# Transformer block with mLSTM and differential attention: second q and k groups and their heads ahead of convolutions and cells, idle steps behind GpSimd's roots, and w_out's first two sums kept outside PSUM

## The chip, the cores and the metric

The kernel runs on one core of a Trainium2 chip. The metric is the device time of one execution in microseconds (us), taken as the median of several runs. A core has TensorE (PE, with its weight loads listed apart as PEld), VectorE (DVE), ScalarE (ACT), GpSimd (POOL) and SyncE (SP); each takes its own instructions in the order in which they were issued, and they wait for each other through semaphores. All loads and stores of this kernel are issued by SyncE.

## What is computed

One block for 256 tokens of width 2048, in fp32. Cut to what matters here:

```
mod = silu(c) @ w_ada + b_ada            # six vectors of 2048
shift1, scale1, gate1, shift2, scale2, gate2 = split(mod, 6)
h = rms_norm(x) * (1 + scale1) + shift1
mq, mk, mv, mo, mi, mf, dq, dk, dv = split(h @ w_in)
mq, mk = silu(causal_dwconv([mq, mk]))                 # 4 taps
h_ml = rms_norm(mlstm_chunkwise(mq, mk, mv, mi, mf)) * sigmoid(mo)   # 4 heads
dq, dk = rope(rms_norm(dq)), rope(rms_norm(dk))        # 8 heads, two maps each
o_da = rms_norm(softmax(q1 k1) @ v - lam * softmax(q2 k2) @ v)
x = x + gate1 * ([h_ml, o_da] @ w_out)
g, u = split((rms_norm(x) * (1 + scale2) + shift2) @ w_gate_up)
out = x + gate2 * ((silu(g) * u) @ w_down)
```

## The kernel before

**Products.** Every large product goes through the same loop. A *tick* is a tile of weights, 128 x 1024. ScalarE copies the raw tile into a rounded high part `wh` (L211 in the profile, the line of the helper `act`), VectorE subtracts it from the raw tile and keeps the low part `wl` (L181, the helper `tt`), and TensorE makes twelve products of 128x128 by 128x512 with it (L581 `wh` by high activations, L582 `wl` by high, L583 `wh` by low), in two half ticks of six. There are 392 ticks: 12 column groups of w_in (two each for attention's q, k and v, one each for the mLSTM's q and k, two each for its v and output gate), w_out with 4 groups of 8, gate_up with 22 groups of 8, down with 4 of 22. Sums stand in two PSUM accumulators (`psA`) of 128 x 1024. All other PSUM work (transposes, scores, small sums) shares four banks (`psM`).

w_in is swept by pairs of k-blocks (`SWEEPS`): the groups in `EARLY` and `LATE` take turns, and a group's sum is added to its `proj` tile after each sweep. `EARLY` is the order of q, k and the mLSTM's q and k: dq0, dk0, mq, mk, dq1, dk1.

**The vectors of w_ada.** 192 tiles of 128 x 1024 are loaded by SyncE, four at a time. A tile is either multiplied by silu(c) and summed on VectorE (`ada`, L185, 128x1024) or used by TensorE (`gv`). `ADA_PLAN` gives for each stage how many tiles are due by which tick; more are taken by `ada_idle` when the planner holds VectorE's queue to be short enough.

**Everything else is woven between the half ticks.** A *work* is a Python generator; each `yield` ends a step and names the PSUM banks that the next step needs. `Plan.run` goes once through the list of works at each half tick, in the order in which they were added, and lets each work whose predecessors are done take one step, as long as the planner's own estimate of the queues of VectorE and ScalarE is below a limit. So the place in the list is a priority, and a step that only yields is a half tick in which that work issues nothing. A tick may need results (`ready`): `mix2` and `mix3`, attention's outputs for w_out's k-blocks 2 and 3, `mix0` and `mix1`, the mLSTM's, for blocks 0 and 1. When they have not been issued at that tick, `Plan.until` steps the works that are needed, and no product is issued in between.

The works near the change, in the order of the list: `q0`, `k0` (`prep`: root mean square, rotary products, eight transposes `tpk`), heads 0 to 3 (`attend`: scores `sc`, softmax `pm`, transposes `aT`; `attend_values`), `mix2` (`finish_attention`: roots `of`, one multiply of the 128x1024 tile `o`, eight transposes `ot`), the convolutions `conv0` and `conv1`, `q1`, `k1`, the cells of pair 0 (`ml_scores` with its score transposes `pp`, `ml_values`, `ml_norm` with its roots `mf`), heads 4 to 7 with `mix3`, the cells of pair 1, then for each pair `mg` (`ml_gate`: a sigmoid of the 128x1024 gate tile on ScalarE) and `mix0`/`mix1` (`ml_out`: four multiplies of `num`, eight transposes `mt`, high copies `mlh` and low parts `mll`), and `rows1` (`gate_rows`: gate1 as rows, four `g1rd` on VectorE and four sums `g1rp` on TensorE).

Reciprocal square roots are made by a first guess on VectorE (`rsqrt_first`) and three Newton rounds of four steps each on GpSimd (`rsqrt_newton`, L401 to L404 in the profile).

**w_out before.** Column groups 0 and 1 first take k-blocks 2 and 3 each, then 0 and 1 each: (g0: 2, 3), (g1: 2, 3), (g0: 0, 1), (g1: 0, 1); groups 2 and 3 follow whole. At the end of each group its sum is read from PSUM, multiplied by gate1's rows and added to x (`residual`, two steps on VectorE), so the last tick of each group needs `rows1`. Behind it stand the squares of the new x for the second norm (`x2_g`).

Of the kernel before, what the change touches and what calls it, by code (L numbers as in the profile page):

```python
# [14 lines left out]
AF = mybir.ActivationFunctionType  # L15
ALU = mybir.AluOpType
# [31 lines left out]
DQ, DK, DV, MQ, MK, MV, MO = (0, 1), (2, 3), (4, 5), 6, 7, (8, 9), (10, 11)  # L48
EARLY = (DQ[0], DK[0], MQ, MK, DQ[1], DK[1])
LATE = (DV[0], DV[1], MV[0], MV[1], MO[0], MO[1])  # L50
# [4 lines left out]
)  # L55
SQ0, SQ1 = True, False
FPAIRS = 6
FSWEEPS = ((0, 2), (2, 5), (5, 8))
# [106 lines left out]
def tile_block(ctx, tc, x, c, pos, par, w_ada, w_in, w_gt, w_out, w_gu, w_dn, out):  # L165
# [8 lines left out]
    plan = Plan()  # L174
# [73 lines left out]
    xs = {}  # L248
# [149 lines left out]

    def rsqrt_newton(y, b, x_):
        for _ in range(3):  # L400
            nc.gpsimd.tensor_tensor(b, y, y, op=ALU.mult)  # L401
            nc.gpsimd.tensor_tensor(b, b, x_, op=ALU.mult)
            nc.gpsimd.tensor_scalar(b, b, -0.5, 1.5, op0=ALU.mult, op1=ALU.add)
            nc.gpsimd.tensor_tensor(y, y, b, op=ALU.mult)  # L404
# [95 lines left out]
    accs = {}  # L500
# [227 lines left out]
    def prep(nm, g):  # L728
# [10 lines left out]
        rsqrt_first(dst, b, xx)  # L739
        rsqrt_newton(dst, b, xx)  # L740
        if nm == "q":
            nc.gpsimd.tensor_scalar(dst, dst, 0.125, None, op0=ALU.mult)
            rope_products(nm, t)
        else:
            yield 0
            v = t.rearrange("p (t m d) -> p t m d", t=2, d=64)
            for k in range(2):
                tt(v[:, k], v[:, k], dst[:, k].unsqueeze(2).to_broadcast([P, 8, 64]), ALU.mult)
            yield 0
            rope_products(nm, t)  # L750
# [80 lines left out]
    def finish_attention(g):  # L831
# [6 lines left out]
        rsqrt_first(f, b, xx)  # L838
        rsqrt_newton(f, b, xx)
        yield 0  # L840
        yield 0
        ov = osl[g].rearrange("p (h d) -> p h d", h=8)
# [149 lines left out]
    def ml_norm(g):  # L992
        h = slice(2 * g, 2 * g + 2)
        yield 0
        stt(mfx[:, h], mden[:, h], -1.0, mden[:, h], ALU.mult, ALU.max)
        tt(mfx[:, h], mfx[:, h], menm[:, h], ALU.max)
        stt(mfx[:, h], mfx[:, h], EPS, mfx[:, h], ALU.mult, ALU.mult)
        stt(mfx[:, h], mssq[:, h], 1.0 / 256, mfx[:, h], ALU.mult, ALU.add)
        rsqrt_first(mf[:, h], mfb[:, h], mfx[:, h])
        rsqrt_newton(mf[:, h], mfb[:, h], mfx[:, h])  # L1000
        yield 0
        yield 0

# [67 lines left out]
    def out_done(g):  # L1071
        def squares():
            yield 0
            for t in range(2):
                square_x(1, g, t)

        def go():
            residual(accs.pop(("wo", g)), rows1, g, xs[g], "o")
            plan.add(f"x2_{g}", squares())
        return go  # L1080
# [132 lines left out]
    mready = lambda kbs: [f"mix{kb}" for kb in kbs]  # L1213
    for g, kbs in ((0, (2, 3)), (1, (2, 3)), (0, (0, 1)), (1, (0, 1))):
        for kb in kbs:
            visit(("wo", g), kb == 2, kb == 1, mix, w_out[g], f"wo{g}", whole((kb,)), mready((kb,)),
                  out_done(g) if kb == 1 else None)
    for g in (2, 3):
# [108 lines left out]
    add_prep(0)  # L1327
    add_heads(0)
    plan.add("conv0", Lazy(conv, 0), fin(MQ))
    plan.add("conv1", Lazy(conv, 1), fin(MK))  # L1330
    add_prep(1)
    add_cells(0)
    add_heads(1)
    add_cells(1)
# [17 lines left out]
    for i, t in enumerate(ticks):  # L1352
# [23 lines left out]
        need = list(t["ready"])  # L1376
        if t["done"] and t["acc"][0] == "wo":
            need.append("rows1")
# [33 lines left out]

ADA_PLAN = ((0, 12, 3), (1, 16, 4), (2, 28, 0), (3, 8, 0), (4, 4, 0), (5, 4, 0), ("wo", 16, 22), ("f0", 24, 5), ("f1", 32, 5), ("f2", 8, 8))

# [70 lines left out]
```

## Time and profile before

| | |
|---|---|
| runs (us) | 1233.88, 1230.26, 1230.19; median 1230.26 |
| profiled execution (us) | 1227.86; its span 1226.1 |
| granted clock, mean | 0.992 |
| busy share: PE, DVE, ACT, POOL | 97%, 69%, 47%, 4% |
| DMA | 313.81 MB, mean 256 GB/s |

The profile is one execution: for each engine what it did when. Of the page, part 1 gives the busy share of each engine, and part 4 the chain of work that ended last, followed back from the last instruction to what released it. The other views are answers of the trace: busy time by stretches of time, groups of instructions by line and tile, the waits of one engine by what ended them, and the timeline, where a row is start, duration, engine, line, operation, output<-inputs, shapes, count, and in brackets the idle time ahead of it and what ended that. The starts of TensorE's products are measured and their ends are modelled.

### The profile page before, as it was taken

What the parts mean: (1) busy time and instruction counts of PE and PEld (TensorE: products, weight loads), DVE (VectorE), ACT (ScalarE), POOL (GpSimd) and SP (SyncE); (2) the same over time, 40 slices, a digit from 0 to 9 for tenths busy, and PEclk for the clock granted to TensorE, in tenths of its full rate; (3) what the DMA queues carried; (4) which work ended last, traced back from release to release, by engine and by line L of the source; (5) the groups of instructions that cost most, each with busy time, mean ns of one, the idle gap of its engine ahead of it and who ended that gap; (6) DMA issues with size and microseconds to landing.
All of it is one profiled execution on the core that took longest, in us unless ns stands there. A gap on an engine that the chain in (4) does not pass through costs nothing.

```text
span 1226.1 us, 14849 instructions
## 1 busy us (share of the span) xinstructions
PE 1189.7 (97%) x5590; PEld 955.9 (78%) x5590; DVE 851.1 (69%) x1197; ACT 582.1 (47%) x791; POOL 50.4 (4%) x126
## 2 busy tenths in 40 slices
PE   6999899998999898999999999999999999999998
PEld 2767678777888686788888888888888878888886
DVE  3757968898888998879856667878555454545443
ACT  3754345565666345665444444444444443433342
POOL 1000001205022000000000000000000000000000
PEclk9999999999999999999999999999999999999999
DMA  9898987656578897899755547998655544646471
GB/s 343 320 363 321 376 324 251 252 207 234 183 257 314 315 355 279 307 337 344 276 186 184 188 169 291 353 351 319 233 178 196 189 172 172 225 169 238 157 257 52
DMA packets 63258, 313.81 MB, mean 256 GB/s; under 512 B 6993, under 2 KB 7377, under 8 KB 41169
## 3 DMA queue, kind: packets, MB, share of 16 engines
q1 hardware_dynamic: 63186, 312.86, 69.9%
q8 instruction: 44, 0.72, 0.2%
q14 instruction: 28, 0.23, 0.0%
HBM read 310.73 MB, written 2.10 MB: 255 GB/s over the span
## 4 chain that ended last, share of the span: by engine, by line
PE 77%; DVE 13%; issue 3%; DMA 2%; POOL 2%; ACT 2%; SPq 0%; DVEq 0%; POOLq 0%; ACTq 0%
DVE wl L181 5%; DVE ada L185 4%; DMA ada<-in_w_ada_dram 2%; PE acc('dn', 0)_7816 L583 2%; PE acc('dn', 0)_7816 L581 2%; PE acc('dn', 2)_8616 L583 2%; PE acc('dn', 2)_8616 L581 2%; PE acc('dn', 1)_8236 L583 2%; PE acc('dn', 1)_8236 L581 2%; PE acc('dn', 0)_7816 L582 2%; PE acc('dn', 2)_8616 L582 2%; PE acc('dn', 1)_8236 L582 2%; DVE proj L181 1%; PE gv L216 1%; PE at L220 1%
## 5 line engine op out<-in xcount | busy, mean ns | idle before, releaser
L181 DVE TENSOR_TENSOR wl<-r,wh 128x1024 fp32r<-128x1024 f32 x392 | 473.6, 1221 | 206.6 <-ACT wh L211 206.3
L211 ACT ACTIVATE wh<-r 128x1024 fp32r<-128x1024 f32 x392 | 410.5, 1058 | 391.3 <-DMA r<-in_w_gu_dram 42.1
L185 DVE SCALAR_TENSOR_TENSOR ada<-ada,silc 128x1024 f32<-128x1024 f32 x152 | 183.0, 1217 | 1.7 <-DMA ada<-in_w_ada_dram 1.7
L216 PE MATMUL gv<-ada,early 128*32 128x256 f32 x320 | 25.7, 424 | 11.9 <-DMA ada<-in_w_ada_dram 11.7
L581 PE MATMUL acc('dn', 0)_7816<-wh,aTh 128*128 128x512 f32 x88 | 35.9, 408 | 0.0
L583 PE MATMUL acc('dn', 0)_7816<-wh,aTl 128*128 128x512 f32 x88 | 34.3, 390 | 0.0
L582 PE MATMUL acc('dn', 0)_7816<-wl,aTh 128*128 128x512 f32 x88 | 34.3, 389 | 0.0
L581 PE MATMUL acc('dn', 1)_8236<-wh,aTh 128*128 128x512 f32 x88 | 34.2, 389 | 0.0
L582 PE MATMUL acc('dn', 1)_8236<-wl,aTh 128*128 128x512 f32 x88 | 34.2, 389 | 0.0
L583 PE MATMUL acc('dn', 1)_8236<-wh,aTl 128*128 128x512 f32 x88 | 34.2, 389 | 0.0
L581 PE MATMUL acc('dn', 2)_8616<-wh,aTh 128*128 128x512 f32 x88 | 34.2, 389 | 0.0
L582 PE MATMUL acc('dn', 2)_8616<-wl,aTh 128*128 128x512 f32 x88 | 34.2, 389 | 0.0
L583 PE MATMUL acc('dn', 2)_8616<-wh,aTl 128*128 128x512 f32 x88 | 34.2, 389 | 0.0
L216 PEld LDWEIGHTS gv<-ada,early 128*32 128x32 f32 x320 | 7.8, 113 | 27.3 <-DMA ada<-in_w_ada_dram 16.4
L211 ACT ACTIVATE hx<-pt,modc,gcol 128x256 f32<-128x256 f32 (+1 forms) x36 | 17.4, 535 | 17.7 <-PE pt L220 14.6
L181 DVE TENSOR_TENSOR hl<-hx,hh 128x512 fp32r<-128x512 f32 (+1 forms) x18 | 11.4, 631 | 18.8 <-ACT hh L211 18.7
L211 ACT ACTIVATE pm<-sc,st,sclq 128x256 f32<-128x256 f32 (+1 forms) x32 | 15.9, 513 | 12.0 <-POOL st L785 12.0
L211 ACT ACTIVATE aTh<-at 128x512 fp32r<-128x512 f32 x22 | 12.0, 596 | 20.0 <-PE at L220 20.0
L211 ACT ACTIVATE fp<-fp 128x1024 f32<-128x1024 f32 x6 | 6.4, 1062 | 29.4 <-DVE fp L181 29.4
L582 PEld LDWEIGHTS acc('dn', 0)_7816<-wl,aTh 128*128 128x128 f32 x88 | 16.5, 188 | 4.2 <-issue 1.0
L581 PEld LDWEIGHTS acc('dn', 0)_7816<-wh,aTh 128*128 128x128 f32 x88 | 16.5, 188 | 4.2 <-issue 1.0
L582 PEld LDWEIGHTS acc('dn', 2)_8616<-wl,aTh 128*128 128x128 f32 x88 | 16.5, 188 | 3.5
(958 smaller groups left out, 2985.9 us busy)
## 6 DMA issues: line engine op xcount, KB each, us to landing
ada<-in_w_ada_dram SPq DMA_DIRECT2D x192, 512.0 KB, 5.7
r<-in_w_gu_dram SPq DMA_DIRECT2D x76, 1024.0 KB, 6.3
r<-in_w_dn_dram SPq DMA_DIRECT2D x44, 1024.0 KB, 4.8
r<-in_w_in_dram SPq DMA_DIRECT2D x36, 1024.0 KB, 6.7
r<-in_w_out_dram SPq DMA_DIRECT2D x16, 1024.0 KB, 7.4
r<-in_w_in_dram SPq DMA_DIRECT2D x24, 512.0 KB, 5.9
r<-in_w_gu_dram SPq DMA_DIRECT2D x24, 512.0 KB, 4.3
x<-in_x_dram SPq DMA_DIRECT2D x4, 512.0 KB, 5.9
```

Of the source, the lines that this page charges most:

```text
L181: nc.vector.tensor_tensor(o, a, b, op=op)
L185: nc.vector.scalar_tensor_tensor(out=o, in0=a, scalar=s, in1=b, op0=op0, op1=op1, accum_out=accum)
L211: nc.scalar.activation(o, a, func, **kw)
L216: nc.tensor.matmul(o, l, r, start=start, stop=stop, **kw)
L220: nc.tensor.transpose(o, a, ident[:])
L581: nc.tensor.matmul(o, ah[:, s], wh[:, r], start=t["start"] and j == 0, stop=False)
L582: nc.tensor.matmul(o, ah[:, s], wl[:, r], start=False, stop=False)
L583: nc.tensor.matmul(o, al[:, s], wh[:, r], start=False, stop=t["stop"] and j == 1)
```

## The change

- `EARLY` becomes dq0, dk0, dq1, dk1, mq, mk. In the list of works `q1`, `k1` and heads 4 to 7 with `mix3` now stand right behind `mix2`, ahead of the convolutions and of all cells.
- `behind(n)` makes a work yield n times without issuing anything. It stands behind the roots of k, of attention's output and of the cells: 7, 7 and 5 for the first group, 1 for the second. Before, these were 1, 2 and 2 steps for both.
- With `now=True`, for these three roots of the second group, the three Newton rounds run as nine steps on VectorE instead of twelve on GpSimd. In the order of instructions GpSimd has 95 rows where it had 131, VectorE 993 where it had 969 (like instructions in a row count once).
- w_out's groups 0 and 1 take turns block by block: 2, 3, 0, 1 of k, and for each g0, then g1. When one of them is complete, ScalarE copies its sum from PSUM into an SBUF slab (`wo0`, `wo1`), and the residual and the squares become a work that waits for `rows1`. Only groups 2 and 3 need `rows1` at their last tick.
- For w_out, `ADA_PLAN` spreads its 16 tiles up to 18 ticks before the stage's end instead of 22.

Line numbers from L57 on are one higher in the changed kernel, and 12 higher from the products on (L593 to L595).

```diff
-EARLY = (DQ[0], DK[0], MQ, MK, DQ[1], DK[1])
+EARLY = (DQ[0], DK[0], DQ[1], DK[1], MQ, MK)
...
+WORDER = (2, 3, 0, 1)
...
+    def behind(n):
+
+        for _ in range(n):
+            yield 0
+
+    def rsqrt_newton(y, b, x_, now=False):
+
         for _ in range(3):
+            if now:
+                tt(b, y, y, ALU.mult)
+                stt(b, b, -0.5, x_, ALU.mult, ALU.mult)
+                stt(y, b, 1.5, y, ALU.add, ALU.mult)
+                continue
...
-        rsqrt_newton(dst, b, xx)
+        rsqrt_newton(dst, b, xx, nm == "k" and g == 1)
...
-            yield 0
+            yield from behind(7 if g == 0 else 1)
...
-        rsqrt_newton(f, b, xx)
-        yield 0
-        yield 0
+        rsqrt_newton(f, b, xx, g == 1)
+        yield from behind(7 if g == 0 else 1)
...
-        rsqrt_newton(mf[:, h], mfb[:, h], mfx[:, h])
-        yield 0
-        yield 0
+        rsqrt_newton(mf[:, h], mfb[:, h], mfx[:, h], g == 1)
+        yield from behind(5 if g == 0 else 1)
...
+        def later():
+
+            kept = slab(f"wo{g}")
+            act(kept[:], accs.pop(("wo", g))[:], AF.Copy)
+            yield 0
+            yield 0
+            residual(kept, rows1, g, xs[g], "o")
+            yield from squares()
+
         def go():
-            residual(accs.pop(("wo", g)), rows1, g, xs[g], "o")
-            plan.add(f"x2_{g}", squares())
+            if g < 2:
+                w = later()
+                next(w)
+                plan.add(f"x2_{g}", w, ["rows1"])
+            else:
+                residual(accs.pop(("wo", g)), rows1, g, xs[g], "o")
+                plan.add(f"x2_{g}", squares())
...
-    for g, kbs in ((0, (2, 3)), (1, (2, 3)), (0, (0, 1)), (1, (0, 1))):
-        for kb in kbs:
-            visit(("wo", g), kb == 2, kb == 1, mix, w_out[g], f"wo{g}", whole((kb,)), mready((kb,)),
-                  out_done(g) if kb == 1 else None)
+    for kb in WORDER:
+        for g in (0, 1):
+            visit(("wo", g), kb == WORDER[0], kb == WORDER[3], mix, w_out[g], f"wo{g}", whole((kb,)), mready((kb,)),
+                  out_done(g) if kb == WORDER[3] else None)
...
     add_prep(0)
     add_heads(0)
+    add_prep(1)
+    add_heads(1)
     plan.add("conv0", Lazy(conv, 0), fin(MQ))
     plan.add("conv1", Lazy(conv, 1), fin(MK))
-    add_prep(1)
     add_cells(0)
-    add_heads(1)
     add_cells(1)
...
-        if t["done"] and t["acc"][0] == "wo":
+        if t["done"] and t["acc"][0] == "wo" and t["acc"][1] >= 2:
...
-ADA_PLAN = (..., ("wo", 16, 22), ...)
+ADA_PLAN = (..., ("wo", 16, 18), ...)
```

What this does to the order shows at three places.

On VectorE, in the part with the attention heads, the end of the first group: `of_269` are the root steps (the last two of the first guess; GpSimd's twelve follow on their own engine), `o` is the 128x1024 multiply that reads their result, `proj_518` and `rpk` are k's normalization and rotary products of the second group, `wl` a weight tile's low part. Before:

```order
L190 TENSOR_SCALAR of_269<-of_269 128x8
L192 TENSOR_SCALAR of_269<-of_269 128x8
L181 TENSOR_TENSOR proj_518<-proj_518,rstk 128x512 x2
L181 TENSOR_TENSOR rpk<-proj_518,rope_kc 128x128 x2
L181 TENSOR_TENSOR rpk<-proj_518,rope_ks 128x128 x2
L181 TENSOR_TENSOR proj_518<-rpk 128x16x8 x2
L181 TENSOR_TENSOR wl_2674<-r_2447,wh_2659 128x1024
L181 TENSOR_TENSOR o_2539<-o_2539,of_269 128x1024
```

After, the last eleven rows up to the same multiply; the first guess ends 27 rows ahead of it. `st` are the maxima of the next heads' scores:

```order
L186 SCALAR_TENSOR_TENSOR ada_5_2_2628,gsum<-ada_5_2_2628,silc_124 128x1024
L182 TENSOR_TENSOR wl_2828<-r_2660,wh_2798 128x1024
L197 TENSOR_REDUCE st_2830<-sc_0_2802 128x1
L197 TENSOR_REDUCE st_2830<-sc_1_2803 128x1
L197 TENSOR_REDUCE st_2830<-sc_0_2802 128x1
L197 TENSOR_REDUCE st_2830<-sc_1_2803 128x1
L197 TENSOR_REDUCE st_2836<-sc_0_2810 128x1
L197 TENSOR_REDUCE st_2836<-sc_1_2811 128x1
L197 TENSOR_REDUCE st_2836<-sc_0_2810 128x1
L197 TENSOR_REDUCE st_2836<-sc_1_2811 128x1
L182 TENSOR_TENSOR o_2586<-o_2586,of_269 128x1024
```

Between the first guess and the multiply there were five rows (nine instructions), and there are 26 now.

On TensorE, in w_out, the transposes `mt` of the first pair of cells, with products of attention's part (`odh`, `odl`) around them. Before:

```order
L583 MATMUL acc('wo', 0)_3396<-wh_3373,odl_3406 128x512
L220 MATMUL mt_3490<-ident,num_2915 128x128 x4
L220 MATMUL mt_3491<-ident,num_2915 128x128 x4
L581 MATMUL acc('wo', 0)_3396<-wh_3424,odh_3405 128x512
L582 MATMUL acc('wo', 0)_3396<-wl_3440,odh_3405 128x512
L583 MATMUL acc('wo', 0)_3396<-wh_3424,odl_3406 128x512
```

The first product that reads `mlh` stands 64 rows further on. After:

```order
L595 MATMUL acc('wo', 1)_3330<-wh_3425,odl_3224 128x512
L221 MATMUL mt_3576<-ident,num_3411 128x128 x4
L221 MATMUL mt_3577<-ident,num_3411 128x128 x4
L593 MATMUL acc('wo', 0)_3252<-wh_3474,mlh_3589 128x512
L594 MATMUL acc('wo', 0)_3252<-wl_3512,mlh_3589 128x512
L595 MATMUL acc('wo', 0)_3252<-wh_3474,mll_3590 128x512
```

The product that reads `mlh` now follows the transposes at once, and the third one reads `mll`.

On VectorE, the same place: `num` are the four multiplies that the transposes read, `mll` the low parts, `modc` and `ada` work for the vectors of w_ada, `g1rd` the diagonals for gate1's rows. Before:

```order
L185 SCALAR_TENSOR_TENSOR num_2915<-num_2915,mf,proj_655 128x256 x4
L181 TENSOR_TENSOR wl_3480<-r_3297,wh_3466 128x1024
L181 TENSOR_TENSOR modc<-gsum 128x16
L181 TENSOR_TENSOR modc<-modc,part 128x16
L185 SCALAR_TENSOR_TENSOR ada_0_1_3287,gsum<-ada_0_1_3287,silc_125 128x1024
L181 TENSOR_TENSOR wl_3511<-r_3297,wh_3488 128x1024
L185 SCALAR_TENSOR_TENSOR num_3343<-num_3343,mf,proj_689 128x256 x4
L185 SCALAR_TENSOR_TENSOR mll_3514<-mt_3490,part,mlh_3513 128x256 x2
L185 SCALAR_TENSOR_TENSOR mll_3514<-mt_3491,part,mlh_3513 128x256 x2
```

After:

```order
L186 SCALAR_TENSOR_TENSOR ada_0_0_3401,gsum<-ada_0_0_3401,silc_124 128x1024
L186 SCALAR_TENSOR_TENSOR ada_0_1_3446,gsum<-ada_0_1_3446,silc_125 128x1024
L182 TENSOR_TENSOR wl_3546<-r_3319,wh_3527 128x1024
L182 TENSOR_TENSOR g1rd_3552<-ident,modc 128x512
L186 SCALAR_TENSOR_TENSOR ada_0_2_3466,gsum<-ada_0_2_3466,silc_124 128x1024
L186 SCALAR_TENSOR_TENSOR num_3411<-num_3411,mf,proj_655 128x256 x4
L186 SCALAR_TENSOR_TENSOR ada_0_3_3504,gsum<-ada_0_3_3504,silc_125 128x1024
L186 SCALAR_TENSOR_TENSOR ada_1_0_3535,gsum<-ada_1_0_3535,silc_124 128x1024
L186 SCALAR_TENSOR_TENSOR ada_1_1_3538,gsum<-ada_1_1_3538,silc_125 128x1024
L186 SCALAR_TENSOR_TENSOR mll_3590<-mt_3576,part,mlh_3589 128x256 x2
L186 SCALAR_TENSOR_TENSOR mll_3590<-mt_3577,part,mlh_3589 128x256 x2
```

Ada steps now stand ahead of `num` and between `num` and `mll`, where a weight split and one ada step stood.

More of the change, by code (lines that the diff above doesn't have):

```diff
@@ L397, in rsqrt_first @@
         ts(y.bitcast(I32), b.bitcast(I32), -1.0, 1597463007.0, ALU.mult, ALU.add)
-    def rsqrt_newton(y, b, x_):
+    def behind(n):
+        for _ in range(n):
+            yield 0
+    def rsqrt_newton(y, b, x_, now=False):
         for _ in range(3):
+            if now:
[3 more added lines that the diff above has]
+                continue
             nc.gpsimd.tensor_tensor(b, y, y, op=ALU.mult)
@@ L1410, in __next__ @@
         return next(self.gen)
-ADA_PLAN = ((0, 12, 3), (1, 16, 4), (2, 28, 0), (3, 8, 0), (4, 4, 0), (5, 4, 0), ("wo", 16, 22), ("f0", 24, 5), ("f1", 32, 5), ("f2", 8, 8))
+ADA_PLAN = ((0, 12, 3), (1, 16, 4), (2, 28, 0), (3, 8, 0), (4, 4, 0), (5, 4, 0), ("wo", 16, 18), ("f0", 24, 5), ("f1", 32, 5), ("f2", 8, 8))
 def _layout(a):
```

## The prediction

> **What bounds the kernel now.** First comes the chain of waits, part 4 of the page: three quarters of the span hang on TensorE (PE). Next the busy times by stretch tell where PE is not filled: 212 to 379 us is the end of the input projection with attention and the mLSTM cells beside it, 379 to 479 is w_out, and after 520 comes the feed-forward part.
>
> ```profile
> PE 77%; DVE 13%; issue 3%; DMA 2%; POOL 2%; ACT 2%; SPq 0%; DVEq 0%; POOLq 0%; ACTq 0%
> ```
>
> ```profile
> 212.00:379.00 167.00, 160.03 (x816) 130.80 (x815) 145.46 (x285) 103.15 (x231) 38.14 (x88) 0.99 0.63 224
> 379.00:479.00 100.00, 96.29 (x417) 76.95 (x415) 92.69 (x141) 48.47 (x68) 5.79 (x12) 0.98 0.90 340
> 520.00:1226.00 706.00, 701.51 (x3137) 579.04 (x3135) 435.64 (x464) 301.65 (x315) 0.00 (x0) 1.00 0.63 228
> ```
>
> The columns are length, busy PE, PEld, DVE, ACT and POOL with their counts, clock, DMA share, GB/s. After 520 us PE issues 3137 products in 706 us, 0.225 us each: that is full speed, and the change touches nothing there. In the two stretches before it VectorE (DVE) is 87% and 93% busy: there it can be the one that is late. The waits of PE from 205 to 520 us, in total, times and longest, name what it was late with:
>
> ```profile
> PE ot L220 <- DVE o L181: 4.2, 1, 4.2
> PE g1rp L216 <- DVE g1rd L181: 3.5, 1, 3.5
> PE acc('gu', 4, 0)_4423 L582 <- DVE wl L181: 1.3, 2, 1.0
> PE tpk L220 <- DVE proj L181: 1.3, 1, 1.3
> PE aT L220 <- ACT pm L211: 0.7, 1, 0.7
> PE sc L216 <- ACT pm L211: 0.5, 1, 0.5
> PE aT L220 <- ACT wh L211: 0.3, 1, 0.3
> ```
>
> These seven rows are the most that the change can win. What each is worth shows in the starts on PE's timeline, since ends are modelled and a stall is followed by a slow stretch:
>
> ```profile
> 225.75 0.39 PE L583 MATMUL acc('in', 7, 4)_1961<-wh,hl 128*128 128x512 f32 x1
> 227.44 1.09 PE L220 MATMUL tpk<-ident,proj 128*128 128x128 f32 x8 [1.29 <-DVE proj L181]
> 228.29 0.48 PE L581 MATMUL acc('in', 7, 4)_1961<-wh,hh 128*128 128x512 f32 x1
> ...
> 302.36 0.39 PE L583 MATMUL acc('in', 5, 2)_2530<-wh,hl 128*128 128x512 f32 x1
> 306.90 1.97 PE L220 MATMUL ot<-ident,o 128*128 128x128 f32 x8 [4.15 <-DVE o L181]
> 308.66 1.55 PE L220 MATMUL tpk<-ident,proj 128*128 128x128 f32 x8
> 309.97 0.48 PE L581 MATMUL acc('in', 5, 2)_2530<-wh,hh 128*128 128x512 f32 x1
> ...
> 414.36 1.02 PE L216 MATMUL g1rp<-g1rd,ones 128*128 128x512 f32 x2
> 418.90 2.02 PE L216 MATMUL g1rp<-g1rd,ones 128*128 128x512 f32 x2 [3.52 <-DVE g1rd L181]
> 419.93 1.42 PE L581 MATMUL acc('wo', 0)_3396<-wh,mlh 128*128 128x512 f32 x1
> 421.14 0.63 PE L582 MATMUL acc('wo', 0)_3396<-wl,mlh 128*128 128x512 f32 x1
> ...
> 422.39 0.39 PE L582 MATMUL acc('wo', 0)_3396<-wl,mlh 128*128 128x512 f32 x1
> ```
>
> Eight transposes by themselves take 0.85 us (227.44 to 228.29), a g1rp 1.02. So k's transposes lost 228.29 - 225.75 - 0.23 - 0.85 = **1.5 us**. Attention's transposes lost 309.97 - 302.36 - 0.23 - 1.7 = **5.7**, of which 1.4 is that the 16 transposes took 3.07 instead of 1.7. The gate rows lost 422.39 - 414.36 - 2.04 - four products at 0.225 = **5.1**.
>
> **Part by part: what goes.** The 4.15 us are GpSimd's: the multiply of o starts when its twelfth root step has ended.
>
> ```profile
> 305.39 0.20 POOL L404 TENSOR_TENSOR of<-of 128x8 f32<-128x8 f32 x1
> ```
>
> ```profile
> 305.62 1.22 DVE L181 TENSOR_TENSOR o<-o,of 128x1024 f32<-128x1024 f32 x1 [1.51 <-POOL of L404]
> ```
>
> With the seven idle steps this multiply stands 26 rows behind the roots in DVE's order, where before it stood five behind; seven of the 26 are 1024 wide, and such steps follow each other at 1.15 us:
>
> ```profile
> 408.86 1.22 DVE L185 SCALAR_TENSOR_TENSOR ada<-ada,silc 128x1024 f32<-128x1024 f32 x1
> 410.01 1.22 DVE L185 SCALAR_TENSOR_TENSOR ada<-ada,silc 128x1024 f32<-128x1024 f32 x1
> ```
>
> That is 8 us of cover from these alone, against a wait of 4.15. I take the 5.7 as gone, and the 1.5 of k in group 0 likewise. The second group's roots run on DVE and need no other engine. The gate rows are no longer awaited where w_out's first group ends, since its sum goes to SBUF: the 5.1 goes. Its price there is two ScalarE copies of 1024, behind which only weight splits queue. The three waits in attention come to 1.5 as listed, some 2 by starts, since a listed idle leaves out about 0.17 of the product's modelled end (0.39 against 0.225). They need not all go: a head's transposes stand 30 to 42 products behind its scores in either order. I take half, 1.1. The 1.3 in the feed-forward part goes too: the fourth block of normed columns is now transposed together with the third, so ScalarE no longer takes it up behind a projection's copy. Together 1.5 + 5.7 + 5.1 + 1.1 + 1.3 = **14.7 us**.
>
> **What comes.** All cells now stand behind all attention heads, so the last score transposes (pp) stand in w_out, and PE has just six products between them and the transposes mt of the first cell pair, and none between mt and the product that reads their result. That chain now stands on the path, twice. Its prices, by groups of DVE and of ACT (count, busy, mean ns, idle before):
>
> ```profile
> L181 DVE TENSOR_TENSOR wl<-r,wh 128x1024 fp32r<-128x1024 f32 x79 | 95.7, 1218 | 1.7 <-ACT wh L211 1.7
> L185 DVE SCALAR_TENSOR_TENSOR ada<-ada,silc 128x1024 f32<-128x1024 f32 x59 | 71.0, 1218 | 1.7 <-DMA ada<-in_w_ada_dram 1.7
> L185 DVE SCALAR_TENSOR_TENSOR num<-num,mf,proj 128x256 f32<-128x256 f32 x8 | 3.3, 478 | 1.5 <-POOL mf L404 1.5
> L185 DVE SCALAR_TENSOR_TENSOR mll<-mt,part,mlh 128x256 fp32r<-128x256 f32 x8 | 3.3, 475 | 0.0
> L181 DVE TENSOR_TENSOR g1rd<-ident,modc 128x512 f32<-128x512 f32 x4 | 2.7, 685 | 0.0
> L185 DVE SCALAR_TENSOR_TENSOR st<-rs,lam,st 128x2 f32<-128x2 f32 x8 | 1.8, 225 | 0.3
> ```
>
> ```profile
> L211 ACT ACT_TABLE_LOAD x6 | 7.7, 1283 | 1.8 <-DVE mneg L196 1.6
> L211 ACT ACTIVATE proj<-proj 128x1024 f32<-128x1024 f32 x2 | 2.0, 1052 | 0.0
> L211 ACT ACTIVATE mp<-pp 128x384 f32<-128x384 f32 x4 | 2.0, 496 | 3.2 <-PE pp L220 3.2
> ```
>
> First stall, ahead of mt: after the last pp ScalarE copies it (0.5), loads a table (1.28), takes the sigmoid (1.05), and DVE multiplies num four times (3.3/2 = 1.65): 4.5. PE has six products, 1.35: **3.1**. DVE's own queue over the same stretch, three ada steps, one split and a g1rd (5.3) with num behind, ends at about the same time, if DVE is some 2.5 us ahead of PE at that pp, which is an estimate from its count of steps up to there. Second stall, behind mt: DVE has three ada steps (3.45) queued ahead of the first mll (0.48); PE has the transposes and two products (1.3): **2.6**. With the slow stretch of 1.4 as behind ot: 3.1 + 2.6 + 1.4 = **7.1**. Second pair: DVE needs two splits, three ada steps, a g1rd, twenty small steps of 0.2 (the root steps that left GpSimd among them) and num, about 12.5 us in all; PE has 46 products at 0.225 and three fp32 blocks of 0.5 to 1, some 11.9: 0.6. Behind its mt again a split and two ada: 2.6. Half a ramp, 0.6. Together **3.8**. On top come thin covers: in group 1 the heads' last transposes, k's and o's each have about 1 us of slack by count; I put **0.7** there.
>
> The bounds: if DVE comes ahead and no ramp follows, the two places cost 4.5 and 2.9, no new stall elsewhere: 7.4. If ada transfers hold DVE, 16 and more. Everything else is hidden: the copies of w_out's sums and two more table loads lie in ScalarE's idle half (48.47 busy of 100), 27 root steps on DVE add 27 x 0.22 = 6 us spread over 200, of which the second pair's nine are counted. On SyncE's queue, which issues all loads, weights and ada tiles keep their order among themselves, but more tiles are called for in w_out's first half.
>
> One rule speaks about the table load: the Trainium skill, "ScalarE: Activation LUTs", section "What ACT_TABLE_LOAD costs", adds a drain of about 1.38 us to each switch. By it the first stall would be 1.4 longer and the change worth 1.7 instead of 3.1. The trace does not show it: six loads here have 1.8 us of idle ahead in all, not 8.
>
> The sum: 11.6 - 14.7 = **-3.1 us**. It is made against the profiled execution of 1227.86 us (span 1226.1), so 1224.8; the runs shown have a median of 1230.26, and I predict **1227.0** beside that. A measurement of this kernel tells about 0.3%, 3.7 us, from no change, so the forecast lies just inside that edge.
>
> **The rivals.**
> A, cheap chains. DVE reaches num early and the clock holds: the new stalls cost 7.4, the sum is -7.3, 1223. For it: the planner issues nothing new while it waits for a mix, so queues are short. Against it: the ramp follows shorter stalls in this trace, below. Chance 0.21.
>
> ```profile
> 164.79 0.64 PE L216 MATMUL gv<-ada,early 128*32 128x256 f32 x8 [1.78 <-DMA ada<-in_w_ada_dram]
> ...
> 167.27 0.63 PE L581 MATMUL acc('in', 9, 2)_1444<-wh,hh 128*128 128x512 f32 x1
> 167.70 0.63 PE L582 MATMUL acc('in', 9, 2)_1444<-wl,hh 128*128 128x512 f32 x1
> ```
>
> Here products follow at 0.43, half speed, behind a wait of 1.78. The Trainium skill, "TensorE: Matmul & The Clock Gate", Part 1, has the rate halved after an idle window of about 3.4 us. By that rule stalls of 3.1 and 2.6 would leave full speed and save 2.0, a sum of -5.1; the rows above disagree with it, so I leave the ramp in.
>
> B, attention gets tight. Heads of both groups now run back to back, ScalarE and DVE alternate in them, and four PSUM banks serve all: if each of the four or five thin covers fails by 1 us, 4 to 5 us come back as waits of aT, tpk or ot on DVE and ACT. Then the sum is +1 to +2 and the time 1231, no change. The idle steps would do nothing that shows. For it: DVE at 87% already. Against: today's longest wait of aT or sc is 0.7. Chance 0.16.
>
> C, slower: the ada tiles. w_out already has the DMA rings at a share of 0.90 and 340 GB/s. The change calls for eleven tiles between the last pp and the second mll. DVE takes its queue in order, so a tile that has not landed holds num and mll behind it, and with them PE. It decides from the point where the new stalls pass 14.7 + 3.7 = 18.4. At one tile per 2.0 to 2.3 us instead of 1.2 (an estimate: 0.52 MB of tile with as much of weights beside it takes 3.1 us at 340 GB/s) eleven tiles are 9 to 12 us late: a sum of +6 to +9, say 1237. Against it: DVE waited 1.7 us in all for ada in 205 to 480 us. Chance 0.13.
>
> **How the numbers follow.** The forecast has 0.50 and a range of its own from 1223.5 to 1230; half of it lies under 1226.6, where faster begins. Faster: 0.25 + 0.21 = 0.46. Same: 0.25 + 0.16 = 0.41. Slower: 0.13. The range runs from 1220, for A with the attention waits gone too, to 1234, where C begins; it leaves out C and a little of A.
>
> **What would show it.** Right: in the waits of PE, ot and g1rp are gone, and two new rows stand at mt on num and at w_out's products on mll, 2 to 3 us each, with products at 0.43 behind them; POOL has 36 steps fewer. A shows as these rows under 1.5 us, B as new rows of aT, tpk or ot, C as DVE rows ada<-DMA of several us between pp and mll. I am wrong if ot or g1rp still stand there, or if the feed-forward part differs by more than 2 us.

## Result and profile after

The changed kernel takes 1221.89 us (median of 4 runs, 1221.63 to 1223.18) against 1232.07 us for the kernel before beside it: a ratio of 0.9918, with an interval from 0.9903 to 0.9933, so 8 to 12 us faster. A second comparison, below, gave 0.9939 (0.9919 to 0.9960). The profiled executions stand closer together: 1227.86 before, 1223.18 after (spans 1226.1 and 1221.5), 4.7 us.

Where the two traces part shows in the starts of the same products: the first of the last sweep over the groups in `EARLY`, the first of w_out's third group (nearly everything that the change moves lies between these two), and the first of gate_up's second sweep. Before, then after:

```profile
186.87 0.39 PE L581 MATMUL acc('in', 0, 4)_1621<-wh,hh 128*128 128x512 f32 x1
...
435.13 0.39 PE L581 MATMUL acc('wo', 2)_3846<-wh,odh 128*128 128x512 f32 x1
...
553.57 0.48 PE L581 MATMUL acc('gu', 0, 2)_4790<-wh,hh 128*128 128x512 f32 x1
```

```profile
188.96 0.39 PE L593 MATMUL acc('in', 0, 4)_1621<-wh,hh 128*128 128x512 f32 x1
...
432.12 0.39 PE L593 MATMUL acc('wo', 2)_3847<-wh,odh 128*128 128x512 f32 x1
...
548.94 0.39 PE L593 MATMUL acc('gu', 0, 2)_4798<-wh,hh 128*128 128x512 f32 x1
```

| stretch | before | after | difference |
|---|---|---|---|
| up to the first row | 186.87 | 188.96 | +2.1 |
| first to second row | 248.26 | 243.16 | -5.1 |
| second to third row | 118.44 | 116.82 | -1.6 |
| from there to the end of the span | 672.5 | 672.6 | 0 |

The first 2.1 us are most likely not the change's. Ahead of this row it only swaps the order of four groups in each sweep, and the row's start varies from one execution to the next: over all profiles of this case it lies between 185.73 and 189.53 in the nine with the old `EARLY` and between 185.67 and 189.88 in the five with the new one. TensorE waits for tiles of w_ada there, 7.8 to 11.7 us in all, but these listed waits alone do not explain the order of the starts. So behind that point the change wins 6.7 us. In the second profile of each kernel (below) the start is 186.58 and 188.62, and the two stretches are 4.7 and 1.6 us shorter after the change: 6.3 us.

The waits of PE from 205 to 520 us after the change, in total, times and longest (a row of pt with 0.7 is left out):

```profile
PE acc('wo', 0)_3252 L595 <- DVE mll L186: 2.8, 2, 2.3
PE acc('gu', 0, 0)_4207 L593 <- ACT hh L212: 2.2, 2, 1.1
PE mt L221 <- DVE num L186: 2.1, 1, 2.1
PE po L217 <- ACT pm L212: 0.7, 1, 0.7
...
```

The rows of ot, g1rp, tpk and aT are gone. Two new ones stand at the first pair of cells, mt on num and w_out's products on mll. (The row of hh stood before too, with the same 2.2.) On PE's timeline the place reads:

```profile
390.04 1.46 PE L217 MATMUL nu<-proj,mp 128*128 128x256 f32 x6
391.14 0.58 PE L593 MATMUL acc('wo', 1)_3330<-wh,odh 128*128 128x512 f32 x1
...
395.57 0.40 PE L595 MATMUL acc('wo', 1)_3330<-wh,odl 128*128 128x512 f32 x1
398.10 1.82 PE L221 MATMUL mt<-ident,num 128*128 128x128 f32 x8 [2.14 <-DVE num L186]
399.61 0.80 PE L593 MATMUL acc('wo', 0)_3252<-wh,mlh 128*128 128x512 f32 x1
400.21 0.63 PE L594 MATMUL acc('wo', 0)_3252<-wl,mlh 128*128 128x512 f32 x1
403.12 0.79 PE L595 MATMUL acc('wo', 0)_3252<-wh,mll 128*128 128x512 f32 x1 [2.29 <-DVE mll L186]
...
404.57 0.63 PE L595 MATMUL acc('wo', 0)_3252<-wh,mll 128*128 128x512 f32 x1
404.99 2.18 PE L217 MATMUL nu<-proj,mp 128*128 128x256 f32 x6
407.01 1.02 PE L217 MATMUL g1rp<-g1rd,ones 128*128 128x512 f32 x2
...
418.31 1.03 PE L221 MATMUL mt<-ident,num 128*128 128x128 f32 x8
...
420.67 0.50 PE L595 MATMUL acc('wo', 0)_3252<-wh,mll 128*128 128x512 f32 x1 [0.48 <-DVE mll L186]
421.01 0.39 PE L593 MATMUL acc('wo', 0)_3252<-wh,mlh 128*128 128x512 f32 x1
```

From 395.57 to 407.01 PE did seven products (0.225 each), eight transposes (0.85) and six nu (1.10, from the first two rows): 3.5 us of work in 11.4, **7.9 lost**. The products in between follow at 0.42 to 0.43, and the nu take 2.02: half speed up to 407 us. In the second profile of this kernel the same stretch loses 8.5. The second pair has only the 0.48 and little beside it: from 418.31 to 421.01 three products and eight transposes take 2.7 where 1.5 would do, **1.2 lost**.

VectorE at the same place shows why. It waits for the sigmoid ahead of num, and then three ada steps stand ahead of mll. The last row is num of the second pair, which is not late:

```profile
397.56 1.67 DVE L186 SCALAR_TENSOR_TENSOR num<-num,mf,proj 128x256 f32<-128x256 f32 x4 [2.46 <-ACT proj L212]
399.15 1.22 DVE L186 SCALAR_TENSOR_TENSOR ada<-ada,silc 128x1024 f32<-128x1024 f32 x1
...
400.30 1.22 DVE L186 SCALAR_TENSOR_TENSOR ada<-ada,silc 128x1024 f32<-128x1024 f32 x1
...
401.44 1.22 DVE L186 SCALAR_TENSOR_TENSOR ada<-ada,silc 128x1024 f32<-128x1024 f32 x1
...
402.59 0.88 DVE L186 SCALAR_TENSOR_TENSOR mll<-mt,part,mlh 128x256 fp32r<-128x256 f32 x2
...
415.12 1.67 DVE L186 SCALAR_TENSOR_TENSOR num<-num,mf,proj 128x256 f32<-128x256 f32 x4
```

ScalarE's part of that chain, behind the last pp:

```profile
394.61 0.49 ACT L212 ACTIVATE mp<-pp 128x384 f32<-128x384 f32 x1
395.10 1.28 ACT L212 ACT_TABLE_LOAD   x1
396.39 1.06 ACT L212 ACTIVATE proj<-proj 128x1024 f32<-128x1024 f32 x1
```

The table load begins as the copy ends and the sigmoid as the load ends: 1.28 us and no more. The drain of about 1.38 us that the Trainium skill, "ScalarE: Activation LUTs", section "What ACT_TABLE_LOAD costs", adds to it is not there.

### The profile page after: what moved, and what is told of

It reads as the page before. It is cut to its first block, busy times and chain, and to the rows that moved or that the text cites. A ratio compares the mean times of both kernels' runs of the same rounds, so it can differ in the third digit from the quotient of the medians.

```text
span 1221.5 us, 14863 instructions
## 1 busy us (share of the span) xinstructions
PE 1192.5 (98%) x5590; PEld 957.5 (78%) x5590; DVE 856.2 (70%) x1224; ACT 586.2 (48%) x795; POOL 41.8 (3%) x90
## 4 chain that ended last, share of the span: by engine, by line
PE 87%; DVE 7%; DMA 3%; issue 2%; ACT 1%; SPq 0%; POOL 0%; DVEq 0%; ACTq 0%; POOLq 0%
DMA ada<-in_w_ada_dram 3%; DVE ada L186 2%; DVE wl L182 2%; PE acc('dn', 0)_7811 L595 2%; PE acc('dn', 0)_7811 L594 2%; PE acc('dn', 2)_8611 L594 2%; PE acc('dn', 2)_8611 L593 2%; PE acc('dn', 1)_8231 L594 2%; PE acc('dn', 1)_8231 L593 2%; PE acc('dn', 1)_8231 L595 2%; PE acc('dn', 0)_7811 L593 2%; PE acc('dn', 2)_8611 L595 2%; PE gv L217 1%; PE at L221 1%; PE apart('dn', 3)_8992 L594 1%
## 5 line engine op out<-in xcount | busy, mean ns | idle before, releaser
L182 DVE TENSOR_TENSOR wl<-r,wh 128x1024 fp32r<-128x1024 f32 x392 | 474.4, 1223 | 207.5 <-ACT wh L212 206.6
L186 DVE SCALAR_TENSOR_TENSOR ada<-ada,silc 128x1024 f32<-128x1024 f32 x152 | 183.2, 1220 | 0.0
L593 PE MATMUL acc('dn', 0)_7811<-wh,aTh 128*128 128x512 f32 x88 | 35.9, 408 | 0.0
L595 PE MATMUL acc('dn', 0)_7811<-wh,aTl 128*128 128x512 f32 x88 | 34.3, 390 | 0.0
L594 PE MATMUL acc('dn', 0)_7811<-wl,aTh 128*128 128x512 f32 x88 | 34.3, 389 | 0.0
L593 PE MATMUL acc('dn', 1)_8231<-wh,aTh 128*128 128x512 f32 x88 | 34.2, 389 | 0.0
L594 PE MATMUL acc('dn', 1)_8231<-wl,aTh 128*128 128x512 f32 x88 | 34.2, 389 | 0.0
L595 PE MATMUL acc('dn', 1)_8231<-wh,aTl 128*128 128x512 f32 x88 | 34.2, 389 | 0.0
L593 PE MATMUL acc('dn', 2)_8611<-wh,aTh 128*128 128x512 f32 x88 | 34.2, 389 | 0.0
L594 PE MATMUL acc('dn', 2)_8611<-wl,aTh 128*128 128x512 f32 x88 | 34.2, 389 | 0.0
L595 PE MATMUL acc('dn', 2)_8611<-wh,aTl 128*128 128x512 f32 x88 | 34.2, 389 | 0.0
L182 DVE TENSOR_TENSOR hl<-hx,hh 128x512 fp32r<-128x512 f32 (+1 forms) x18 | 11.4, 631 | 16.0 <-ACT hh L212 15.8
L593 PEld LDWEIGHTS acc('dn', 0)_7811<-wh,aTh 128*128 128x128 f32 x88 | 16.5, 188 | 4.3 <-issue 1.0
```

The lines of the kernel that those rows point to most:

```text
L182: nc.vector.tensor_tensor(o, a, b, op=op)
L186: nc.vector.scalar_tensor_tensor(out=o, in0=a, scalar=s, in1=b, op0=op0, op1=op1, accum_out=accum)
L593: nc.tensor.matmul(o, ah[:, s], wh[:, r], start=t["start"] and j == 0, stop=False)
L594: nc.tensor.matmul(o, ah[:, s], wl[:, r], start=False, stop=False)
L595: nc.tensor.matmul(o, al[:, s], wh[:, r], start=False, stop=t["stop"] and j == 1)
```

## The experiments

Each ran beside the kernel before on one chip; ratios are to that. The waits shown are those of PE behind 205 us.

**The kernel before again.** No edit.

> The kernel before, unchanged, to see what varies from one execution to the next. Theory (steady stalls): the waits at ot (4.2 us) and at g1rp (3.5 us) stand in this second profile too, within 0.5 us, and what varies between executions lies ahead of 205 us, where TensorE waits for tiles of w_ada. Rival (a stall that comes and goes): an execution of 1230 us or more shows a further wait of 2 us or more behind 205 us, which the profile of 1227.9 us did not have, and the change gains more than its profile shows because that wait is gone.

Measured: 1.0006 (0.9994 to 1.0017); twelve runs from 1228.11 to 1235.04 with a median of 1230.89, the profiled one 1228.11, their fastest. Its waits behind 205 us:

```profile
PE ot L220 <- DVE o L181: 4.1, 1, 4.1
PE g1rp L216 <- DVE g1rd L181: 3.9, 1, 3.9
```

Both stalls stand as they did, with no further one. The rival has no support, but no execution over 1230 us was profiled, so it is not refuted: what the slower executions of this kernel wait for stays open.

**Idle steps alone.** The kernel before with

```diff
-            yield 0
+            for _ in range(7 if g == 0 else 1):
+                yield 0
...
-        rsqrt_newton(f, b, xx)
-        yield 0
-        yield 0
+        rsqrt_newton(f, b, xx)
+        for _ in range(7 if g == 0 else 2):
+            yield 0
```

and the same with 5 and 2 behind the cells' roots.

> The kernel before with only the idle steps behind the first group's roots (7, 7 and 5). Theory (terms of the prediction): the losses at ot (5.7 us) and at k's transposes (1.5 us) go, so -7 us; two half ticks are now forced for mix3 and give up to 2 us back: -5 to -7, 0.9943 to 0.9959 of before, and no ot row above 0.5 us for the first group. Rival (attention tight): the steps only move the wait to other transposes of the heads, less than 2 us gained, new rows of aT, tpk or po of 1 us and more.

Measured: 0.9929 (0.9915 to 0.9943), 1221.97 us. Its waits of PE, cut to those that changed:

```profile
PE pt L220 <- DVE hx L190: 2.5, 1, 2.5
...
PE tpk L220 <- DVE proj L181: 1.7, 1, 1.7
PE sc L216 <- ACT pm L211: 1.6, 1, 1.6
...
PE acc('wo', 0)_3367 L583 <- DVE odl L185: 0.7, 1, 0.7
...
PE g1rp L216 <- DVE g1rd L181: 0.5, 1, 0.5
```

ot is gone, and the steps by themselves win some 9 us. But g1rp is down from 3.5 to 0.5 as well: the rows show that the gate rows are nearly in time here, and not why. Transposes of attention and cells that stood ahead of w_out now stand in its first products, which wait for attention (0.7 at odl); that this gives the gate rows their time is not shown. So most of the wait at g1rp goes by either edit. And the second group's k (tpk) and scores now wait, with w_out's first products, and pt ahead of gate_up waits 2.5 where it waited 1.3: the direction of the theory held, its figure was somewhat small (8.4 by the medians against 5 to 7) and its list was not right.

**Sums outside PSUM alone.** The kernel before with the new `out_done` (see the change) and

```diff
-        if t["done"] and t["acc"][0] == "wo":
+        if t["done"] and t["acc"][0] == "wo" and t["acc"][1] >= 2:
```

w_out's order unchanged.

> The kernel before with only w_out's first two sums copied to SBUF and their residuals made later, in the old order of w_out. Theory (terms of the prediction): the loss of 5.1 us ahead of g1rp goes and nothing comes in its place: -5 us, 0.996 of before. Rival (deferred): the residuals and squares of groups 0 and 1 crowd VectorE and ScalarE later, g1rp or the wait ahead of gate_up comes out later by as much, less than 2 us gained.

Measured: 0.9925 (0.9910 to 0.9941), 1222.13 us, more than the 5 expected. Its trace, with ot as before:

```profile
PE ot L220 <- DVE o L181: 4.1, 1, 4.1
...
PE acc('gu', 11, 0)_4726 L582 <- DVE wl L181: 1.0, 1, 1.0
...
PE pt L220 <- DVE hx L190: 0.7, 1, 0.7
```

g1rp is gone. In starts, w_out's first to third group takes 50.65 us (381.63 to 432.28) where it took 56.07 (379.06 to 435.13): 5.4 us, the term of 5.1. Further, pt ahead of gate_up falls from 1.3 to 0.7, and the wait on wl in gate_up goes from group 4 to group 11. No wait on the residuals or squares came in its place.

**The old place of the heads.** The changed kernel with

```diff
-EARLY = (DQ[0], DK[0], DQ[1], DK[1], MQ, MK)
+EARLY = (DQ[0], DK[0], MQ, MK, DQ[1], DK[1])
...
-    add_prep(1)
-    add_heads(1)
     plan.add("conv0", Lazy(conv, 0), fin(MQ))
     plan.add("conv1", Lazy(conv, 1), fin(MK))
+    add_prep(1)
     add_cells(0)
+    add_heads(1)
     add_cells(1)
```

> The changed kernel with the old place of q1, k1 and heads 4 to 7 in the list and the old EARLY; idle steps, roots on VectorE, sums outside PSUM and w_out's block order stay. Theory (late cells cost): no half tick is forced for mix0 or mix1, so the waits of mt on num (2.1 us) and of w_out on mll (2.3 us) with the slow products behind them, 8.4 us by starts in the changed kernel's trace, go for the most part: 5 to 8 us faster than the changed kernel, 0.985 to 0.988 of before. Rival (the heads' order is where the gain is): waits of aT, sc and ot come back in the heads, as slow as the changed kernel or slower by 2 to 5 us.

Measured: 0.9850 (0.9833 to 0.9867), 1212.83 us. Its waits of PE, beside those for hh (as before) and pt (0.7, as in the changed kernel) ahead of gate_up:

```profile
PE sc L217 <- ACT pm L212: 0.7, 1, 0.7
...
PE aT L221 <- DVE pm L186: 0.6, 1, 0.6
```

mt and mll wait no more, and nothing comes back in the heads but 0.7 and 0.6. The edit named first in the change's title is the one that costs.

Both were run once more, on one chip:

> The changed kernel once more, for a direct comparison on one chip. Theory: 0.9918 to 0.994 of before, with the waits of mt on num and of w_out on mll at 2 to 2.5 us each, as in the first profile.

> The changed kernel with the old place of q1, k1 and heads 4 to 7, once more beside the changed kernel. Theory (the new place of the heads costs what the late cells wait for): 7 to 10 us faster than the changed kernel, 0.984 to 0.987 of before. Rival (the first result was a good chip hour): within 4 us of it.

Measured: the changed kernel 0.9939 (0.9919 to 0.9960), 1222.64 us, with mt at 2.1 and mll at 2.1; the one with the old heads 0.9867 (0.9843 to 0.9891), 1214.17 us. 8.5 us between them: the rival falls. (The expectations put the loss at the first pair at 8.4 by starts; by the rows above it is 7.9.) In the traces the two kernels part by 9.7 to 10.6 us behind the first row of the table.

**No idle steps in the changed kernel.**

Behind k's roots, attention's and the cells', in this order:

```diff
-            yield from behind(7 if g == 0 else 1)
+            yield from behind(1)
...
-        yield from behind(7 if g == 0 else 1)
+        yield from behind(2)
...
-        yield from behind(5 if g == 0 else 1)
+        yield from behind(2)
```

> The changed kernel with the idle steps taken back to 1, 2 and 2 for both groups; everything else of the change stays. Theory (the idle steps with the new list order make the cells late): cells come two ticks earlier, no half tick is forced for mix0 and mix1, the waits at mt and mll (8.4 us by starts) go, and the waits at ot (5.7) and tpk (1.5) of the first group come back: within 3 us of the changed kernel. Rival (late cells are the doing of the list order alone): mt and mll stay as they are and ot and tpk come on top, 5 to 8 us slower than the changed kernel, no better than 0.997 of before.

Measured: 0.9930 (0.9910 to 0.9949), 1222.53 us, level with the changed kernel. Its longest waits of PE:

```profile
PE aT L221 <- ACT wh L212: 3.0, 1, 3.0
PE tpk L221 <- DVE proj L182: 2.2, 2, 1.3
...
PE sc L217 <- ACT pm L212: 2.1, 2, 1.9
```

mt and mll are gone, as the theory had it, but ot did not come back: in VectorE's order four maxima of the next head, an ada step and a weight split stand between the first guess of the roots and the multiply even so, since those heads now come right behind `mix2`. What comes is aT, sc and tpk in the heads; ScalarE is named as late for aT and sc, VectorE for tpk. So taking the idle steps out wins in w_out about what it loses in the heads. Whether these waits are the price of the new place of the heads or of the missing idle steps is not shown: the old heads without idle steps, with the rest of the change, were not run.

**No ada steps while half ticks are forced.**

```diff
-        plan.until(need, lambda: ada_idle(VFORCE))
+        plan.until(need, lambda: None if t["acc"][0] == "wo" else ada_idle(VFORCE))
```

> The changed kernel, but no ada steps are issued while half ticks are forced for mix0 and mix1; so none of them stands between num and mll in VectorE's order (three did), and one fewer ahead of other steps. Theory (VectorE's queue makes the second stall): the wait of w_out on mll, 2.3 us, falls under 0.5, and 2 to 4 us are gained with the slow products behind it. Rival (the copies mlh on ScalarE set it): the wait stays over 1.5 us, less than 1 us gained.

Measured: 0.9930 (0.9911 to 0.9949), 1222.31 us. Its waits of PE on num and mll:

```profile
PE mt L221 <- DVE num L186: 2.1, 1, 2.1
...
PE acc('wo', 0)_3252 L595 <- DVE mll L186: 0.6, 1, 0.6
```

The wait of the first pair on mll is gone (the 0.6 is the second pair's), so VectorE's queue made it. The wait of mt and half speed behind it stay. By its spans the trace is 2.7 us shorter than the changed kernel's (1218.8 against 1221.5); the runs cannot tell the two apart.

**The sigmoid earlier.** `ml_gate` without its wait for the cells' scores:

```diff
-fin(MO[g]) + [f"at{h}" for h in range(8)] + [f"ms{h}" for h in range(4)]
+fin(MO[g]) + [f"at{h}" for h in range(8)]
```

> The changed kernel with the sigmoid of the gate tile allowed before the last scores of the cells. Theory (table load and sigmoid behind the last pp make the first stall): VectorE, which waited 2.5 us for the sigmoid ahead of num, goes on at once, and the wait of mt falls from 2.1 us to about 0.7 (one ada step more stands ahead of it by then); 1 to 2 us gained. Rival (num waits for the roots or VectorE is late itself): the wait of mt stays at 2 us or more.

Measured: 0.9929 (0.9908 to 0.9949), 1221.93 us. The same two rows of its waits:

```profile
PE acc('wo', 0)_3252 L595 <- DVE mll L186: 5.0, 2, 2.8
...
PE mt L221 <- DVE num L186: 0.9, 1, 0.9
```

mt falls to 0.9, near the 0.7 expected, but the 1 to 2 us are not won. The three ada steps keep their place, and the first pair waits 2.8 for mll where it waited 2.3. Behind that wait the products follow at 0.23, full speed, so PE comes early to the second pair, and waits 2.2 there for mll where it waited 0.5. The first link of the chain was read rightly; cutting it alone hands the wait to the next.

**What the rest of the change does.** Three kernels with the old heads, idle steps and sums outside PSUM. The first is the kernel before with these two edits alone, as above: roots on GpSimd, the old order of w_out's blocks, margin 22.

> The kernel before with the idle steps and the sums outside PSUM and nothing else: roots on GpSimd, old w_out order, old heads, ADA_PLAN at 22. Theory (these two edits carry the gain and add up): -8 and -9 us as each had alone, 16 to 18 us faster than before, 0.985 to 0.987, level with the kernel with the old heads. Rival (roots on VectorE and the block order matter): the second group's ot and w_out's first products on odh and odl wait 1 to 3 us each, 0.988 or more of before.

Measured: 0.9908 (0.9888 to 0.9927), 1220.14 us. The theory falls: 9 and 9 do not make 18, since both edits take the same g1rp, and the second group's waits are left. In the traces, from the first row of the table to w_out's third group, idle steps alone are 7.0 us shorter than before, sums alone 4.3 and both together 7.9.

The other two are the kernel with the old heads, one with all roots on GpSimd, one with the old order of w_out's blocks:

```diff
-        rsqrt_newton(dst, b, xx, nm == "k" and g == 1)
+        rsqrt_newton(dst, b, xx)
...
-        rsqrt_newton(f, b, xx, g == 1)
+        rsqrt_newton(f, b, xx)
...
-        rsqrt_newton(mf[:, h], mfb[:, h], mfx[:, h], g == 1)
+        rsqrt_newton(mf[:, h], mfb[:, h], mfx[:, h])
```

```diff
-    for kb in WORDER:
-        for g in (0, 1):
+    for g, kb in ((0, 2), (0, 3), (1, 2), (1, 3), (0, 0), (0, 1), (1, 0), (1, 1)):
```

> The kernel with the old heads, and all roots on GpSimd again; w_out's block order stays. It differs from idle steps and sums alone (0.9908) by the block order. Theory (second group's roots cost waits on GpSimd): tpk and sc of the second group wait 1 to 2 us each as in that kernel, 0.988 to 0.990. Rival (the block order alone makes the difference): odh and odl wait no longer, as fast as the old heads with roots on VectorE, 0.984 to 0.987.

> The kernel with the old heads, roots on VectorE, and w_out's groups 0 and 1 in the old order (2, 3 of one, then of the other). Two half ticks are forced for mix3. Theory (roots): w_out's first products wait about 1 us in all for odh and odl, the rest is as with the old heads: 0.985 to 0.988. Rival (block order): 0.989 or more, with waits of 2 us and more at w_out's first products.

Measured: roots on GpSimd with the new block order 0.9918 (0.9896 to 0.9940), 1219.75 us; roots on VectorE with the old order 0.9881 (0.9861 to 0.9901), 1215.42 us; beside them all parts with the old heads, 0.9867. In the waits of PE, with the roots on GpSimd:

```profile
PE pt L221 <- DVE hx L191: 2.5, 1, 2.5
...
PE tpk L221 <- DVE proj L182: 1.6, 1, 1.6
PE sc L217 <- ACT pm L212: 1.6, 1, 1.6
```

And with the old block order:

```profile
PE acc('wo', 0)_3340 L595 <- DVE mll L186: 1.2, 1, 1.2
PE acc('wo', 0)_3340 L595 <- DVE odl L186: 1.1, 1, 1.1
```

By the runs the roots on VectorE are worth 5.6 us and the block order 1.3, which the intervals do not separate from nothing, though its waits are plain in the trace. Behind the first row of the table the traces have 8.2 and 4.6.

Not all of the 8.2 is a wait for roots. Some 3.8 lie ahead of w_out's third group, where tpk and sc wait. The other 4.4 lie behind it, where pt waits 2.5 for VectorE (0.7 with the roots on VectorE) and the products behind it follow at 0.43; the kernel with idle steps and sums alone, with all its roots on GpSimd too, has only 0.7 there. So this part comes of the order in VectorE's queue, and how that hangs on the roots was not followed.

The kernel with the roots on GpSimd differs from that with idle steps and sums alone in two more things than the block order: the margin of `ADA_PLAN` (18 for 22) and one idle step behind two roots of the second group. Neither the margin nor that step was run by itself.

## Why the prediction was right, and where its sizes were off

- **The direction and the mechanism held.** ot and g1rp left the waits, two rows came at mt on num and at w_out's products on mll with products at 0.43 behind them, GpSimd lost 36 steps, and the part behind gate_up's first sweep is the same to 0.1 us. By the traces' own account the forecast of -3.1 stands against -4.7, or -6.7 without the start. By the runs it stands against -10.2: 1221.89 lies in the whole range of 1220 to 1234, but outside the forecast's own 1223.5 to 1230. The mechanism was read rightly and the size was not; that the time still lies in the range is owed to the range's width.
- **Gone, forecast 14.7.** The 5.1 of the gate rows measured 5.4 with that edit alone; ot's and tpk's rows are gone; the three attention waits are gone, and one of 0.7 came at po. The 1.3 in the feed-forward part was wrong: it was put down to the third and fourth block being transposed together, but the wait on wl leaves its place with the sums alone, where they are not, and comes back with 1.0 in gate_up's group 11. Nor were the seven rows "the most that the change can win": the same view of before has two more, hh with 2.2 and pt with 1.3, and pt fell to 0.7. The whole stretch from w_out's third group to gate_up's second sweep won 1.6.
- **Come, forecast 7.1 + 3.8 + 0.7.** The first pair cost 7.9. By starts its two gaps took 2.3 and 2.7, near the 3.1 and 2.6; half speed lasted through both of them and took the other 2.9, where 1.4 was laid out. The second pair cost 1.2 instead of **3.8, the mis-sized term**: mt did not wait at all. VectorE's 12.5 us of work were right: from the end of the first pair's mll (404.15) to that of num (416.71) it took 12.6. PE's 11.9 were not: from the product that reads mll (403.12) to the second mt (418.31) it took 15.2, in part at half speed, up to 407 us. So VectorE was 1.6 us ahead at mt, which took most of the 2.6 behind it too, and no slow stretch followed. With 9.1 come and 6.7 won, some 15.8 must have gone, where 14.7 was forecast: the sum missed by 2.5 in what comes and 1.1 in what goes.
- **Rival A's figure, 1223, came nearest, but not by A.** Its stalls were to be under 1.5 us and without the slow stretch; they were 2.1 and 2.3, with it. Nor did its reason hold that the planner issues nothing new while it waits for a mix: the run without ada steps in forced half ticks shows that three of them came from there, ahead of mll. B's rows of aT, tpk and ot did not come at all. C's decider did not come: ahead of VectorE's ada steps no time was lost to tiles. The group in 205 to 480 us, with the idle time before it last:

```profile
L186 DVE SCALAR_TENSOR_TENSOR ada<-ada,silc 128x1024 f32<-128x1024 f32 x61 | 73.7, 1221 | 0.0
```

- **From the trace to the runs.** The prediction set its sum against the profiled execution and subtracted it from the median (which gives 1227.2, not the 1227.0 that it names). The medians of the two comparisons lie 10.2 and 7.1 us apart, the two pairs of profiled executions 4.7 and 4.3: both executions of before (1227.86 and 1228.11) are faster than nearly all its other runs, both of after (1223.18 and 1223.85) slower than most of theirs. Behind the first row the pairs part by 6.7 and 6.3, which the second comparison agrees with. The start ahead of it varies by 4 us between profiles, enough for the rest, but what the other runs wait for was not profiled, so this stays open.
- **Not seen.** The prediction priced the roots on VectorE only as 27 steps of 0.22 us and never as what they take off the path. With the old heads they are worth 5.6 us by the runs, and by the traces some 3.8 us at the places that wait for them. And it read the change as one thing, where one part loses 8.5 of what the others win: the version with the old heads, 1213 to 1214 us, beats both kernels.

## What to carry to other kernels

Before moving work ahead in a priority list, ask whose work is then last, and whether anything lies between that and the product that needs it: here, with the idle steps in place, the heads gained nothing by coming first, and the cells' chain of copy, table load, sigmoid, multiply and transposes came to stand bare. Two edits that remove the same stall cannot be added; try them alone and together. And a single profile of each kernel is not the median: set its time among the other runs before a difference of a few microseconds is read from a pair.

## What the runs showed of the hardware

In the two profiles of the kernel before, PE waited 1.78 and 1.79 us at the same place, near 165 us; in the first the products behind it follow at 0.43 from the fifth on, as the prediction showed, in the second at full speed throughout:

```profile
165.67 0.64 PE L216 MATMUL gv<-ada,early 128*32 128x256 f32 x8 [1.79 <-DMA ada<-in_w_ada_dram]
...
168.19 0.39 PE L583 MATMUL acc('in', 9, 2)_1444<-wh,hl 128*128 128x512 f32 x1
168.41 0.39 PE L581 MATMUL acc('in', 9, 2)_1444<-wh,hh 128*128 128x512 f32 x1
```

From the gv to the first product behind the eight transposes that follow, the same work took 6.2 us in the first (164.79 to 170.99) and 4.6 in the second (165.67 to 170.28): the same wait costs 1.6 us more or not from one execution to the next. Nor does the length of the wait alone decide. At this place a wait of 1.26 us, in the first profile of the changed kernel, was followed by products at 0.43; a wait of 2.98 at aT without idle steps, and one of 2.79 at mll with the sigmoid earlier, were followed by products at 0.23.

The Trainium skill, "TensorE: Matmul & The Clock Gate", Part 1, describes a free-running window of about 3.4 us whose activity sets the rate. That the outcome changes from run to run agrees with it. That it takes an idle window to halve the rate does not, unless more than the listed waits counts as idle, since waits of 1.3 to 2.3 us did it here; beside them PE had only short work, such as sixteen gv in the 3.9 us between two large products (161.50 to 165.36), and what the window makes of that no run here shows.
